# A hybrid decoder layer: the products of C and B of all groups in one place, and two attention pairs' transposes ahead of the next scores

## The chip, the cores and the metric

The kernel runs on one core of one Trainium2 chip. The metric is the device time of one execution in microseconds. Each of the core's engines runs its own queue in order and meets the others at semaphores: TensorE (PE; its weight loads are listed as PEld), VectorE (DVE), ScalarE (ACT), GpSimd (POOL) and SyncE (SP). Here SyncE only issues the loads of weights.

## The reference

One layer over 256 tokens of width 1024, in float32: a SwiGLU block, a mixer, a second SwiGLU block, with RMSNorm ahead of and behind each. The change lies in the mixer, which has two branches that share one input projection:

```python
z, xbc, dt_raw, q, k, v, gate_logits = split(u @ w_in)
# branch 1: state-space duality, in 2 chunks of 128 tokens, 4 groups of 8 heads
xs, bm, cm = split(silu(causal_dwconv(xbc)))
CB = einsum('bclgn,bcsgn->bgcls', C, B)          # per group g and chunk c
y_diag = einsum('bgcls,bgecls,bcsgep->bclgep', CB, Lmat, X)
# branch 2: differential attention, 8 heads with 2 maps each
p = softmax(q @ k.T * scale - slopes * dist)     # causal
out = (p[:, :, 0] - lam * p[:, :, 1]) @ v
out = rmsnorm(out, subln_g) * (1 - lam_init)
merged = gates[0] * (y_ssd @ w_a) + gates[1] * (out @ w_b)
h = h + rmsnorm(merged @ w_out)
```

Two steps matter here. `CB` is, for each of the four groups, a product of that group's C and B (128 states) for all pairs of tokens; the kernel computes the two diagonal blocks and the one below the diagonal. The attention's output of a pair of heads has to be transposed, so that it can be the stationary operand of its output projection.

## The kernel before, in words

**Large products.** All weights are streamed from memory in chunks of 1 MB. Each chunk is split into a high part (ScalarE, L168) and a low part (VectorE, L171) of a faster 32-bit format, and each large product is the sum of three: high by high, low by high and high by low (`mm_t` at L197, `mm_nat` at L225). Three chunks are split ahead of the one in use. The mixer's chunks come in this order: V, B and C, X (8 chunks, tile `pxs`), Z (8, `pz`), Q and K (8), the gates (8, `pgt`), the first branch's projection (8, `pws`), the second's (4, `pwd`), the output's (4). A chunk of the X stage is 48 products of 256 columns; a half-chunk of the later stages is 12 products of 512 columns.

**Small products.** Between the large ones TensorE has small ones in plain float32, each of which shows as two rows in the trace: the products of C and B (`pcb`, L865 and L866), the transposes of X (`px`) and the products of a group (`py`), and in attention the scores (`psc`, L986 and L987), the transposes of the weights of a head (`pa`, L1021), the values (`po`, L1033 to L1035) and the transposes of a pair's output (`pto`, L1060). Their results share a pool of five PSUM buffers with the tag `bg` (L84); the large products have three of their own, with the tag `pj` (L77). A tile that finds no free buffer waits until the last reader of an older tile is done.

**What sets the order.** The small work is written as generators: `cb_work` (L862), `ssd_work` (L875), `ssd_norm` (L924) and `att_work` (L1077). Each yields an estimate in microseconds after a step. A `Background` (L1109) takes steps from the first generator in its list while it has credit; the main program gives it credit after each chunk or half-chunk (`back.run`, 0.4 after an X chunk, 1.35 or 1.55 after a half-chunk of the gates and of the first branch's projection). A `BREAK` ends a call early. So the estimates decide between which large products the small ones stand. TensorE's order is the order of the program from there on; ScalarE's and VectorE's orders are chosen by the framework's scheduler.

**The products of C and B before.** One step of `cb_work` is one group: a new `bg` tile, its two products, VectorE's multiplication with the causal mask (L867), and an estimate of 0.5. With 0.4 of credit after each X chunk, one group runs after each of the first four X chunks. B and C come from a convolution (`conv`, L822): ScalarE's first tap (L826), VectorE's three further taps (L829), and ScalarE's Silu (L261). C's second half, which groups 2 and 3 read, is the last one to come out of it before X.

**Attention before.** `att_work` runs in rounds n = 0 to 5 over pairs of heads. A round has, where they exist: the scores and the softmax of pair n; the transposes of pair n-1's weights; the combination of the two maps of pair n; then, after a break, the values of pair n-1 and the norm of its output (`Pair.norm`, L1044); and last the transposes of pair n-2's output (`Pair.turn`, L1056), which ScalarE (L1072) and VectorE (L1073) read out as the high and low operand of the projection.

Of the kernel before, what the change touches and what calls it, by code (L numbers as in the profile page):

```python
# [24 lines left out]
P = 128  # L25
# [6 lines left out]
H_ATT = 8  # L32
# [16 lines left out]
def tile_hybrid_layer(ctx: ExitStack, tc: tile.TileContext, x, ffn1_pre_g, ffn1_w_gate, ffn1_w_up,  # L49
# [4 lines left out]
    nc = tc.nc  # L54
# [5 lines left out]
    def k4(shape, name, dt=F32):  # L60
        return sb.tile(shape, dt, tag="k4", name=name, bufs=K4_BUFS)
# [21 lines left out]
    def bg(shape, name):  # L83
        return ps.tile(shape, F32, tag="bg", name=name, bufs=5)  # L84
# [166 lines left out]
    order = mybir.DependencyInfo(mybir.DependencyClass.NoSync, mybir.DependencyReason.DATA)  # L251
# [68 lines left out]
    for name, v in (("mx", mix_pre_g), ("f2", ffn2_pre_g),  # L320
                    ("ng", ssd_norm_g), ("cb", ssd_conv_b), ("sg", da_subln_g)):
        n = v.shape[1] // P
# [447 lines left out]
    for jj in range(2):  # L770
        for a in (uh, ul):
            for i in range(4):
                k = i * 2 + jj
                nc.tensor.matmul(pdt[i * H_SSD:(i + 1) * H_SSD, :], wdt[:, k, :], a(k).bitcast(F32),
                                 start=jj == 0 and a is uh, stop=jj == 1 and a is ul)
# [73 lines left out]
    bT = k4([P, 4, T], "bT")  # L849
    cT = k4([P, 4, T], "cT")  # L850
# [9 lines left out]
    cbm = [cbm2[g // 2][:, g % 2, :] for g in range(4)]  # L860

    def cb_work():  # L862
        for g in range(4):
            pc = bg([P, 3 * P], f"pcb{g}")
            nc.tensor.matmul(pc[:, P:], bT[:, g, :P], cT[:, g, :], start=True, stop=True)  # L865
            nc.tensor.matmul(pc[:, :P], bT[:, g, P:], cT[:, g, P:], start=True, stop=True)  # L866
            nc.vector.tensor_tensor(cbm[g], pc, m3.rearrange("p a b -> p (a b)"), ALU.mult)  # L867
            yield 0.5

# [207 lines left out]
    def att_work():  # L1077

        pairs = [Pair(hp) for hp in range(H_ATT // 2)]
        heads = [Head(hd, pairs[hd // 2]) for hd in range(H_ATT)]
        for n in range(H_ATT // 2 + 2):
            here, old = heads[2 * n:2 * n + 2], heads[2 * n - 2:2 * n] if n else []
            for head in here:
                head.scores()
            for head in here:
                head.softmax()
                yield 2.3
            for head in old:  # L1090
                head.turn()
            if old and opens:
                opens.pop()()
            for head in here:
                head.combine()
                yield 1.3
            yield BREAK
            if old:
                for head in old:
                    head.values()  # L1100
                pairs[n - 1].norm()
                yield 1.8
                if n == H_ATT // 2:
                    yield BREAK
            if n >= 2:
                pairs[n - 2].turn()
                yield 0.8

# [25 lines left out]

    back = Background()
    back.add(cb_work())
    for g in range(4):
        xs[g] = k4([P, 4, T], f"xs{g}")
# [19 lines left out]
    for c in range(4):  # L1158
# [11 lines left out]
        back.run(BG_US)  # L1170

    back.add(att_work())


# [126 lines left out]
```

## Time and profile before

| | |
|---|---|
| time, median of 3 runs | 743.7 us (743.64 to 743.83) |
| the profiled execution, device time | 743.95 us |
| its span in the profile | 742.2 us |
| TensorE busy | 734.1 us (99%) |
| VectorE busy | 525.2 us (71%) |
| ScalarE busy | 441.1 us (59%) |
| GpSimd busy | 38.0 us (5%) |
| read from memory | 136.17 MB, 185 GB/s over the span |
| the products of C and B | between 249.0 and 269.1 us of the span |
| the transposes of pairs' outputs | between 470.0 and 505.2 us of the span |

The profile shows one execution. A row of its order of time gives the start in microseconds from the span's start, the duration in microseconds, the engine, the line of the kernel, the operation, the tile that is written and those that are read, the shape, and the number of instructions that are merged into the row; in brackets, the time that the engine sat idle before it and what ended that. A matrix product's duration overlaps with the next one's, so what a product costs is read from the distance between starts. A row of the list of waits gives who waited for whom: microseconds in total, times, and the longest.

### The profile page before, as it was taken

To read this page: it belongs to the slowest core of one execution; us is meant where nothing else is said; L and a number is where in the kernel's file an instruction comes from. 1 tells how busy PE (TensorE), PEld (TensorE's weight loads), DVE (VectorE), ACT (ScalarE), POOL (GpSimd) and SP (SyncE) were. 2 spreads that over 40 slices of the span, in tenths; PEclk is the share of its full clock that TensorE was granted. 3 is DMA by queue.
4 is the path that set the end of the run, shared out by engine and by line. 5 is a ranking of instruction groups with operands and counts; after the bars stand their busy time and mean duration, and the time that the engine had idled before them with its cause. 6 is when DMAs were issued, how large, how long until landed. Compare 5 with 4: busy or idle time off the path is not lost.

```text
span 742.2 us, 11061 instructions
## 1 busy us (share of the span) xinstructions
PE 734.1 (99%) x4369; PEld 641.7 (86%) x4369; DVE 525.2 (71%) x807; ACT 441.1 (59%) x742; POOL 38.0 (5%) x72
## 2 busy tenths in 40 slices
PE   8999999999999999999999999999999999999996
PEld 7888888888889999999999888888888888888885
DVE  6986567654577888787878997684775857766612
ACT  6665557553566565959957656772664655665512
POOL 2700000000300000000000000000020000000000
PEclk9999999999999999999999999999999999999998
DMA  8884666487253647666556455374470777645701
GB/s 291 232 261 150 213 227 254 170 286 226 64 169 118 192 150 225 191 186 223 170 161 217 165 178 213 118 244 182 140 243 15 227 226 227 193 172 185 273 1 57
DMA packets 94212, 137.96 MB, mean 186 GB/s; under 512 B 2684, under 2 KB 68304, under 8 KB 94160
## 3 DMA queue, kind: packets, MB, share of 16 engines
q1 hardware_dynamic: 91488, 129.51, 53.0%
q0 software_dynamic: 2368, 7.22, 3.1%
q8 instruction: 34, 0.56, 0.3%
q10 hardware_dynamic: 304, 0.53, 0.2%
q14 instruction: 18, 0.15, 0.1%
HBM read 136.17 MB, written 1.08 MB: 185 GB/s over the span
## 4 chain that ended last, share of the span: by engine, by line
PE 98%; DMA 1%; issue 0%; DVE 0%; SPq 0%; DVEq 0%; ACT 0%
PE acc_f L470 16%; PE pup_f L219 9%; PE pg_f L219 9%; PE pws L234 6%; PE pgt L234 6%; PE pg_f L218 4%; PE pup_f L218 4%; PE pn_f L244 3%; PE pn_f L234 3%; PE acc_mx L470 3%; PE pn_mx L234 3%; PE pwd L234 3%; PE pz L205 2%; PE pxs L207 2%; PE pz L207 2%; PE pxs L205 2%
## 5 line engine op out<-in xcount | busy, mean ns | idle before, releaser
L171 DVE TENSOR_TENSOR wlo<-raw,whi 128x1024 fp32r<-128x1024 f32 (+1 forms) x246 | 291.0, 1212 | 56.1 <-ACT whi L168 54.8
L168 ACT CAST whi<-raw 128x1024 fp32r<-128x1024 f32 (+1 forms) x245 | 246.8, 1045 | 55.4 <-PE acc_f L470 19.6
L219 PE MATMUL pg_f<-u_f,whi 128*128 128x512 f32 x288 | 101.3, 396 | 0.0
L219 PE MATMUL pup_f<-u_f,whi 128*128 128x512 f32 x288 | 101.1, 396 | 0.0
L218 PE MATMUL pg_f<-u_f,wlo 128*128 128x256 f32 x252 | 70.6, 280 | 0.0
L218 PE MATMUL pup_f<-u_f,wlo 128*128 128x256 f32 x252 | 70.3, 279 | 0.0
L219 PEld LDWEIGHTS pg_f<-u_f,whi 128*128 128x128 f32 x288 | 52.8, 188 | 9.7
L219 PEld LDWEIGHTS pup_f<-u_f,whi 128*128 128x128 f32 x288 | 52.7, 188 | 9.8
L470 PE MATMUL acc_f<-whi,gh_f 128*128 128x512 f32 x176 | 58.2, 390 | 0.0
L470 PE MATMUL acc_f<-whi,gl_f 128*128 128x512 f32 x176 | 58.1, 389 | 0.0
L470 PE MATMUL acc_f<-wlo,gh_f 128*128 128x512 f32 x176 | 58.1, 389 | 0.0
L218 PEld LDWEIGHTS pg_f<-u_f,wlo 128*128 128x128 f32 x252 | 47.5, 189 | 1.8
L218 PEld LDWEIGHTS pup_f<-u_f,wlo 128*128 128x128 f32 x252 | 47.5, 189 | 1.6
L223 DVE TENSOR_TENSOR su_f<-pup_f,su_f 128x256 f32<-128x256 f32 x36 | 15.2, 422 | 40.4 <-ACT su_f L222 40.4
L470 PEld LDWEIGHTS acc_f<-whi,gl_f 128*128 128x128 f32 x176 | 33.0, 188 | 6.9
L470 PEld LDWEIGHTS acc_f<-wlo,gh_f 128*128 128x128 f32 x176 | 33.0, 188 | 6.8
L470 PEld LDWEIGHTS acc_f<-whi,gh_f 128*128 128x128 f32 x176 | 33.0, 188 | 6.8
L234 PE MATMUL pgt<-whi,u_mx 128*128 128x512 f32 x128 | 33.1, 393 | 0.0
L222 ACT COPY su_f<-pup_f 128x256 f32<-128x256 f32 x36 | 13.4, 372 | 31.4 <-PE pup_f L219 31.1
L204 PE MATMUL pxs<-u_mx,whi 128*128 128x256 f32 x128 | 31.7, 285 | 0.0
L205 PE MATMUL pz<-u_mx,whi 128*128 128x256 f32 x128 | 31.6, 284 | 0.0
L204 PE MATMUL pz<-u_mx,whi 128*128 128x256 f32 x128 | 31.6, 284 | 0.0
(310 smaller groups left out, 1432.7 us busy)
## 6 DMA issues: line engine op xcount, KB each, us to landing
raw<-in_w_in_dram SPq DMA_DIRECT2D x40, 1024.0 KB, 5.4
raw<-in_ffn_w_down_dram SPq DMA_DIRECT2D x22, 1024.0 KB, 5.5
raw<-in_ffn_w_gate_dram SPq DMA_DIRECT2D x20, 1024.0 KB, 5.7
raw<-in_ffn_w_up_dram SPq DMA_DIRECT2D x20, 1024.0 KB, 5.4
raw<-in_ssd_w_branch_dram SPq DMA_DIRECT2D x8, 1024.0 KB, 5.0
acb<-acd POOLq DMA_DIRECT2D x8, 512.0 KB, 5.3
raw<-in_da_w_branch_dram SPq DMA_DIRECT2D x4, 1024.0 KB, 5.1
raw<-in_w_out_dram SPq DMA_DIRECT2D x4, 1024.0 KB, 5.0
```

The source lines that it names most:

```text
L168: copy(hi[:, js, :], r[:, q * nj + j:q * nj + j + n, :])
L171: nc.vector.tensor_sub(lo[:, js, :], r[:, q * nj + j:q * nj + j + n, :], hi[:, js, :].bitcast(F32))
L204: nc.tensor.matmul(acc[m], wh(j)[:, cs], ah(k0 + j), start=first and j == ks[0], stop=False)
L205: nc.tensor.matmul(acc[m], wh(j)[:, cs], al(k0 + j), start=False, stop=False)
L207: nc.tensor.matmul(acc[m], wl(j)[:, cs], ah(k0 + j), start=False, stop=last and j == ks[-1])
L218: nc.tensor.matmul(acc[:, :T], wl(j)[:, cs], ah(j), start=False, stop=False)
L219: nc.tensor.matmul(acc, wh(j)[:, cs], ahl(j), start=j == 0, stop=j == KD - 1)
L222: nc.scalar.copy(dst[:, m, :], acc[:, T:])
L223: nc.vector.tensor_tensor(dst[:, m, :], acc[:, :T], dst[:, m, :], ALU.add)
L234: nc.tensor.matmul(acc, a(k0 + j), b(j), start=first and i == 0, stop=last and i == 11)
L244: nc.tensor.matmul(accs[b], x_(k0 + j), w_(j), start=first and j == 0 and w_ is wh and x_ is acts[b][0], stop=last and j == 3 and w_ is wl)
L470: nc.tensor.matmul(acc[b][q], x_[:, ts], w_(kt)[:, halves[q]], start=i == 0 and kt == 0 and x_ is ah and w_ is wh, stop=i == n - 1 and kt ...
```

## The change

The products of C and B: `cb_work` now takes all four `bg` tiles first and issues the eight products one behind the other, held in that order by dependencies without a semaphore; then come the four masks, each with the same estimate of 0.5 as before.

Attention: for rounds 3 and 4 the transposes of pair n-3 stand at the start of the round, ahead of the scores, and no longer at the end of the round before. An estimate of 0.8 after them is gone, and the estimate after each of the two softmaxes is 2.7 in place of 2.3 from round 3 on. Pairs 2 and 3 are transposed at the end of rounds 4 and 5, as before.

```diff
     def cb_work():
-        for g in range(4):
-            pc = bg([P, 3 * P], f"pcb{g}")
-            nc.tensor.matmul(pc[:, P:], bT[:, g, :P], cT[:, g, :], start=True, stop=True)
-            nc.tensor.matmul(pc[:, :P], bT[:, g, P:], cT[:, g, P:], start=True, stop=True)
+        pcs = [bg([P, 3 * P], f"pcb{g}") for g in range(4)]
+        last = None
+        for g, pc in enumerate(pcs):
+            for m in (nc.tensor.matmul(pc[:, P:], bT[:, g, :P], cT[:, g, :], start=True, stop=True),
+                      nc.tensor.matmul(pc[:, :P], bT[:, g, P:], cT[:, g, P:], start=True, stop=True)):
+                if last is not None:
+                    tc.add_manual_dep(m.ins, last.ins.name, order, reason="together")
+                last = m
+        for g, pc in enumerate(pcs):
             nc.vector.tensor_tensor(cbm[g], pc, m3.rearrange("p a b -> p (a b)"), ALU.mult)
             yield 0.5
...
         for n in range(H_ATT // 2 + 2):
             here, old = heads[2 * n:2 * n + 2], heads[2 * n - 2:2 * n] if n else []
+            if 3 <= n <= H_ATT // 2:
+                pairs[n - 3].turn()
             for head in here:
                 head.scores()
             for head in here:
                 head.softmax()
-                yield 2.3
+                yield 2.3 if n < 3 else 2.7
...
-            if n >= 2:
+            if n >= H_ATT // 2:
                 pairs[n - 2].turn()
                 yield 0.8
```

## The prediction

> **What bounds the kernel now.** I read the page's first part, the slices and the chain that ended last, and then the list of waits for TensorE alone.
>
> ```profile
> span 742.2 us, 11061 instructions
> PE 734.1 (99%) x4369; PEld 641.7 (86%) x4369; DVE 525.2 (71%) x807; ACT 441.1 (59%) x742; POOL 38.0 (5%) x72
> ...
> PEclk9999999999999999999999999999999999999998
> ...
> PE 98%; DMA 1%; issue 0%; DVE 0%; SPq 0%; DVEq 0%; ACT 0%
> ```
>
> ```profile
> PE warm L310 <- POOL ident L296: 1.6, 1, 1.6
> PE pn_f L244 <- DVE whi L168: 0.2, 1, 0.2
> ```
>
> TensorE holds 98% of the chain at the full granted clock, and the only two waits that the list has for it lie in the first microseconds. So a microsecond taken from TensorE's own stream, or a wait put into it, goes straight to the end; what moves on VectorE and ScalarE costs nothing until TensorE waits for it. The question is therefore what TensorE's stream saves, and which dependency that had slack is now met too early.
>
> **What the change does to the queues.** I compared the instruction order in which the two programs are built. TensorE's order differs in two places alone: the products of C and B of groups 1, 2 and 3 (L865, L866) move up behind those of group 0, and the scores of heads 6 and 7 (L986, L987) move up over one half-chunk of 12 products (L234), so that they follow pair 0's transposes (L1060) directly. The transposes of pairs 1, 2 and 3 stay where they were, so most of the second part's wording changes nothing. Counts are the same: no instruction is added or removed. POOL's and SyncE's orders are the same, so no DMA is moved past another. VectorE and ScalarE change in a few neighbouring places in the two stretches.
>
> **Part 1: the four groups together, what it saves.** TensorE's order of time around group 0, then the starts of groups 1 and 2, then a stretch without such a group:
>
> ```profile
> 249.03 0.60 PE L865 MATMUL pcb<-cT,bT 128*128 128x256 f32 x2
> 249.47 0.38 PE L866 MATMUL pcb<-cT,bT 128*128 128x128 f32 x2
> ...
> 249.81 0.28 PE L205 MATMUL pxs<-u_mx,whi 128*128 128x256 f32 x1
> ...
> 255.44 0.60 PE L865 MATMUL pcb<-cT,bT 128*128 128x256 f32 x2
> ...
> 261.85 0.60 PE L865 MATMUL pcb<-cT,bT 128*128 128x256 f32 x2
> ...
> 273.70 1.12 PE L207 MATMUL pxs<-u_mx,wlo 128*128 128x256 f32 x8
> 276.58 1.12 PE L207 MATMUL pxs<-u_mx,wlo 128*128 128x256 f32 x8
> ```
>
> Without a group, 24 products take 276.58 - 273.70 = 2.88 us, 0.12 each, so a full chunk of 48 takes 5.76. With one it takes 255.44 - 249.03 = 6.41. A group costs 0.65. Its own stream is 0.44 (249.03 to 249.47) for the two wide passes and 0.22 for the two narrow ones (the price of two narrow passes in the order of time below, 469.79 to 470.01), together 0.66. So going into the group and back costs nothing that these rows show, and three exits fewer save 0.00. The upper bound of a switch is the 0.09 of part 2.
>
> **Part 1: the wait it adds.** Group 2 reads the second half of C. It is final after its Silu (L261), which stands in ScalarE's queue behind the first step of the next convolution (L826); the third row is from the order of weight loads:
>
> ```profile
> 249.23 0.57 ACT L826 ACTIVATE xs<-pxs,cols_a,cols_b 128x256 f32<-128x256 f32 x1 [1.90 <-PE pxs L207]
> 249.70 0.62 ACT L261 ACTIVATE cT<-cT 128x512 f32<-128x512 f32 x1
> ...
> 249.69 0.19 PEld L205 LDWEIGHTS pxs<-u_mx,whi 128*128 128x128 f32 x1
> ```
>
> The Silu ends at 249.70 + 0.62 = 250.32. Before, group 2 ran at 261.85 and had 11 us to spare; now its first product comes at 249.03 + 2 x 0.65 = 250.33, and its weight load, which carries the wait, starts some 0.11 earlier (a load at 249.69 for the product of 249.81 shows that lead in the rows after the group), at 250.22. A release takes 0.05:
>
> ```profile
> 574.94 0.69 DVE L573 TENSOR_TENSOR sg_f2b<-pn_f,sg_f2b 128x512 f32<-128x512 f32 x1
> ...
> 575.68 0.66 PE L581 MATMUL pt_f<-ident,sg_f2b 128*128 128x128 f32 x4
> ```
>
> (VectorE ends at 575.63, TensorE starts at 575.68). So the load starts at 250.37 instead of 250.22: +0.15. Ends: 0 if that Silu ends 0.15 sooner, and 0.4 if the load is no longer hidden behind a product (0.19 on top). I take 0.15. Behind it wait groups 2 and 3 and the next chunk of X; VectorE's masks (L867) come earlier than before, and the chunks after group 3's old place are at their old time again, so weight splits only gain time.
>
> **Part 2: what it saves.** TensorE's order of time around pair 0's transposes:
>
> ```profile
> 469.79 0.39 PE L1035 MATMUL po<-v,aT 128*128 128x128 f32 x2
> 470.01 0.60 PE L1060 MATMUL pto<-ident,o 128*128 128x128 f32 x4
> 470.37 1.16 PE L234 MATMUL pws<-whi,yh 128*128 128x512 f32 x4
> ...
> 472.27 1.07 PE L234 MATMUL pws<-whi,yl 128*128 128x512 f32 x4
> 473.27 0.50 PE L986 MATMUL psc<-k,q 64*128 64x128 f32 x4
> ...
> 474.03 0.49 PE L986 MATMUL psc<-k,q 64*128 64x128 f32 x4
> ...
> 474.88 1.21 PE L234 MATMUL pws<-whi,yh 128*128 128x512 f32 x4
> ...
> 477.78 1.07 PE L234 MATMUL pws<-whi,yh 128*128 128x512 f32 x4
> ...
> 480.50 1.07 PE L234 MATMUL pws<-whi,yh 128*128 128x512 f32 x4
> ```
>
> Four products of 512 columns take 0.907 (a third of the 2.72 that 12 take from 477.78 to 480.50). The 12 products from 470.37 to 472.27 + 0.91 = 473.18 take 2.81, so leaving the transposes for products cost at most 0.09; most of that is only the first row being stamped early. The scores start 0.09 after 473.18 because their tile changes to 64 rows; that price stays, whatever stands ahead. One exit fewer saves between 0 and 0.09; I take 0.05.
>
> **Part 2: the wait it adds.** The small products share a pool of five buffers (tag bg, L84). In the changed order six of them stand in a row: po of pair 1, pto of pair 0, then the four score tiles of heads 6 and 7. The last one (head 7, second map) must take a buffer back, and in the built program it takes pto's and waits for its last reader, VectorE's L1073 (L1078 in the changed kernel). It did so before as well, but 12 products stood between. The readers:
>
> ```profile
> 470.70 0.68 ACT L1072 ACTIVATE oh<-pto,g 128x512 fp32r<-128x512 f32 x1
> ```
>
> ```profile
> 469.61 1.23 DVE L171 TENSOR_TENSOR wlo<-raw,whi 128x1024 fp32r<-128x1024 f32 x1 [5.97 <-ACT whi L168]
> ...
> 471.44 0.74 DVE L1073 SCALAR_TENSOR_TENSOR ol<-pto,g,oh 128x512 fp32r<-128x512 f32 x1
> ...
> 472.36 2.36 DVE L171 TENSOR_TENSOR wlo<-raw,whi 128x1024 fp32r<-128x1024 f32 x2
> 474.63 0.69 DVE L1054 TENSOR_TENSOR o<-po,ro 128x512 f32<-128x512 f32 x1
> 475.24 0.68 DVE L1216 TENSOR_TENSOR gt<-pws,gt 128x512 f32<-128x512 f32 x1
> 475.83 1.48 DVE L993 SCALAR_TENSOR_TENSOR s<-dneg,psc 128x384 f32<-128x384 f32 x3
> 477.22 0.95 DVE L996 TENSOR_REDUCE nm<-s 128x6 f32<-128x768 f32 x1
> ```
>
> Everything up to L1073 keeps its place in both queues, so it still ends at 471.44 + 0.74 = 472.18 and frees TensorE at 472.23. TensorE is there earlier: transposes end at 470.01 + 4 x 0.11 = 470.45, the tile change adds 0.09, head 6 runs 470.54 to 471.30 (0.76, as 473.27 to 474.03), and head 7's second map would start at 471.31. It waits 0.92. Its four passes then run alone; before, both maps of head 7 shared 0.85 (474.03 to 474.88), and one alone needs between 0.66 (0.22 + 0.44, the group of part 1) and that. So the next product starts between 472.89 and 473.08, and with the transition at 0.09 between 472.98 and 473.08, against 470.54 + 1.61 = 472.15 without a wait: +0.83 to +0.93. I take 0.88. Low end: 0, if L1073 is done in time; high end 1.9, if one ScalarE cast (1.05, the slow rival).
>
> What is late next? VectorE now takes the new scores and the norm before two weight subtractions and before the eviction of the half-chunk (L1216). From 472.25: two scores 0.9 (two thirds of 477.22 - 475.83), the norm 0.6, a maximum 0.9, two subtractions 2.3 and the eviction 0.6 end at about 477.6. TensorE wants that buffer at the product of 480.50, now about 481.5: 3.9 us of cover, and the weight halves that now end some 2 us later are read only after it. Without that cover each extra subtraction would cost its 1.15.
>
> **Sum.** -0.00 +0.15 -0.05 +0.88 = +0.98, say 1.0 us. The profiled execution took 743.95 for its span of 742.2; it becomes 744.95. That execution lies 0.25 above the median of 743.7, so the median becomes 744.7: 0.13% slower, which is inside the 0.2% (1.5 us) that a measurement of this kernel tells from no change.
>
> One rule speaks against this change as a whole. The rows first; in the last, the granted clock is the 1.00 behind the five engines' busy times:
>
> ```profile
> 311.58 2.82 PE L913 MATMUL py<-E,X 128*64 128x256 f32 x32
> 314.33 1.09 PE L881 MATMUL px<-ident,xs 128*128 128x128 f32 x8
> ...
> 311.00:316.00 5.00, 4.98 (x52) 4.02 (x51) 4.15 (x8) 3.79 (x5) 0.00 (x0) 1.00 0.87 257
> ```
>
> A run of small products and transposes of 3.8 us (311.58 to 315.4) left the granted clock at 1.00 in that window. The Trainium skill's page "TensorE: Matmul & The Clock Gate" says in Part 1 that TensorE falls to half its clock after an idle window of about 3.4 us, and in Part 4 that transposes do not count as busy in the same way. By the rows the sum has no term for it; by that rule the longer run here might add an estimated 1.7 us (half of one such window).
>
> **The rivals.**
> (a) The wait at head 7 is not there, because L1073 has already ended: 743.7 + 0.15 - 0.05 = 743.8. Against it: L1073 needs ScalarE's L1072, which cannot start before the transposes end at 470.45 and took until 471.38; then 0.74 alone gives 472.1.
> (b) Slower by more than 0.2%: one 1.05 us cast (L168) comes ahead of L1072, because ScalarE is that much later against TensorE than in this execution, and head 7 waits 1.05 more: 745.8. It decides from 0.5 us of slip on. For it: VectorE's row of 469.61 waited 5.97 us for ScalarE, so this stretch hangs on ScalarE; against it: the order of both queues up to L1073 is fixed and unchanged.
> (c) The clock falls. The run of small work becomes at least 469.79 to 473.0 with a 0.9 us wait in it. If the products after it ran at half speed for as long as that run lasted (3.2), 1.6 us are lost: 746.3. The window from 311 to 316 speaks against it. This is the rule of the Trainium skill's page "TensorE: Matmul & The Clock Gate" that stands above.
> (d) Faster by more than 0.2%: every exit from small products costs far more than the rows say. It takes 1.5 us on four exits, plus the 1.0 of waits: 0.6 each against 0.09 at most; 742.0.
>
> **How the numbers follow.** The forecast has 0.62 (its own range 744.3 to 745.1), (a) 0.12, (b) 0.14, (c) 0.04, (d) 0.05, and 0.03 for another wait that makes it slower. Forecast and (a) are within 0.2%: 0.74. (b), (c) and the rest are slower: 0.21. (d) is faster: 0.05. The range takes in (a) with both savings at their upper bound (743.7 less four exits at 0.09) and (b): 743.3 to 745.9.
>
> **What would show it.** In the profile after: four rows of L866 and L867 in one stretch from 249.03 to about 251.8; a wait of TensorE's pcb on ScalarE's cT of 0.1 to 0.4; a wait of psc on VectorE's L1078 of about 0.9 near 471.4; the granted clock at 1.00; no other wait of TensorE's. The prediction is wrong if that second wait is missing or longer than 1.4, if the clock drops after 473, or if a group of L866 and L867 costs less than 0.6.

## The result: 1.1 us slower, as forecast

The changed kernel takes 744.89 us (median of 20 runs, 744.64 to 745.48). The kernel before takes 743.77 us beside it (median of 20 runs, 743.51 to 744.42). The ratio is 1.0015, with a 95% interval of 1.0009 to 1.0022: 1.12 us or 0.15% slower, where the prediction had 1.0 us and 0.13%. That is inside the 0.2% that the prediction treated as no change, but the interval excludes an equal time.

The page of the changed kernel has the lines that answer to those shown of the kernel before:

```profile
span 742.9 us, 11061 instructions
PE 734.9 (99%) x4369; PEld 642.6 (86%) x4369; DVE 525.6 (71%) x807; ACT 440.8 (59%) x742; POOL 37.9 (5%) x72
...
PEclk9999999999999999999999999999999999999999
...
PE 96%; ACT 1%; DVE 1%; DMA 0%; issue 0%; DVEq 0%
```

TensorE still bounds the kernel, at the full granted clock. What is new is in the last line: the chain that ended last was 98% TensorE before and is 96% now, and for about 1% each it passes through ScalarE and VectorE. All of that is one detour of 18.7 us. In order of time (start, duration, engine, tile and line), its first piece off TensorE, its last one, and the return:

```profile
453.36 1.03 DVE s L998 x2
...
471.34 0.67 DVE ol L1078
...
472.05 0.48 PE psc L991 x2
```

So the share does not tell the size of a wait. The chain shows one wait of TensorE, which ends at 472.05. It is followed back from there through the queues of VectorE and ScalarE, of which only the last microsecond is time that TensorE waited. Around the products of C and B the chain stays on TensorE. The list of waits for TensorE's products has no new row; it has a single one, from the first microseconds:

```profile
PE warm L310 <- POOL ident L296: 1.6, 1, 1.6
```

The weight loads have a list of their own, and there the wait at 472.05 does stand; the list before has no such row:

```profile
PEld psc L991 <- DVE ol L1078: 0.5, 1, 0.5
```

**How the two traces were compared.** Since TensorE's stream is nearly gapless, the distance between the first products of two stages tells what a stage took. The first products of X (`pxs`), of the first branch's projection (`pws`) and of the second's (`pwd`), in TensorE's order of time, before:

```profile
243.27 0.28 PE L204 MATMUL pxs<-u_mx,whi 128*128 128x256 f32 x1
...
449.65 0.70 PE L234 MATMUL pws<-whi,yh 128*128 128x512 f32 x2
...
504.92 0.71 PE L234 MATMUL pwd<-whi,oh 128*128 128x512 f32 x2
```

and after:

```profile
242.93 0.28 PE L204 MATMUL pxs<-u_mx,whi 128*128 128x256 f32 x1
...
449.46 0.70 PE L234 MATMUL pws<-whi,yh 128*128 128x512 f32 x2
...
505.64 0.71 PE L234 MATMUL pwd<-whi,oh 128*128 128x512 f32 x2
```

From `pxs` to `pws`, which holds part 1 of the change, it is 206.38 before and 206.53 after: +0.15. From `pws` to `pwd`, which holds part 2, it is 55.27 and 56.18: +0.91. Together +1.06 us. What lies behind is the same to 0.01 us. What lies ahead is the start-up, which in these two executions happens to be 0.35 shorter after; this is why the profiled span has grown by only 0.7 (1.06 - 0.35). Over many runs that evens out, and the medians are 1.12 apart.

**Part 1.** TensorE's order of time in the changed kernel (L866 and L867 are the old L865 and L866):

```profile
248.69 0.60 PE L866 MATMUL pcb<-cT,bT 128*128 128x256 f32 x2
249.13 0.38 PE L867 MATMUL pcb<-cT,bT 128*128 128x128 f32 x2
249.35 0.60 PE L866 MATMUL pcb<-cT,bT 128*128 128x256 f32 x2
249.78 0.38 PE L867 MATMUL pcb<-cT,bT 128*128 128x128 f32 x2
250.03 0.70 PE L866 MATMUL pcb<-cT,bT 128*128 128x256 f32 x2
250.56 0.38 PE L867 MATMUL pcb<-cT,bT 128*128 128x128 f32 x2
250.79 0.60 PE L866 MATMUL pcb<-cT,bT 128*128 128x256 f32 x2
```

and the Silu of C's second half, in ScalarE's:

```profile
249.36 0.62 ACT L261 ACTIVATE cT<-cT 128x512 f32<-128x512 f32 x1
```

The first group takes 0.66 to the start of the second (248.69 to 249.35). Group 2 starts at 250.03, 0.05 after the Silu's end at 249.98, and takes 0.76 to the next, of which its first row took 0.53 (250.03 to 250.56) where the others take 0.43 or 0.44. The wait shows as a late start (0.02 later than 249.35 + 0.66) and a slower first product, not as idle time: the modelled end of the product before, 249.78 + 0.38 = 250.16, lies beyond it.

**Part 2.** TensorE's order of time around pair 0's transposes, after:

```profile
469.60 0.39 PE L1040 MATMUL po<-v,aT 128*128 128x128 f32 x2
469.82 0.60 PE L1065 MATMUL pto<-ident,o 128*128 128x128 f32 x4
470.35 0.50 PE L991 MATMUL psc<-k,q 64*128 64x128 f32 x4
470.68 0.61 PE L992 MATMUL psc<-k,q 64*128 64x256 f32 x4
471.11 0.38 PE L991 MATMUL psc<-k,q 64*128 64x128 f32 x2
471.33 0.59 PE L992 MATMUL psc<-k,q 64*128 64x256 f32 x2
472.05 0.48 PE L991 MATMUL psc<-k,q 64*128 64x128 f32 x2
472.38 0.59 PE L992 MATMUL psc<-k,q 64*128 64x256 f32 x2
472.90 1.20 PE L234 MATMUL pws<-whi,yh 128*128 128x512 f32 x4
```

and the two readers of pair 0's transposes, on ScalarE and VectorE:

```profile
470.52 0.68 ACT L1077 ACTIVATE oh<-pto,g 128x512 fp32r<-128x512 f32 x1
```

```profile
471.26 0.74 DVE L1078 SCALAR_TENSOR_TENSOR ol<-pto,g,oh 128x512 fp32r<-128x512 f32 x1
```

The count at the end of a `psc` row is what to look at. Head 6 has rows of 4: the products of its two maps run side by side (in the trace each product of the second map starts 0.01 after its partner of the first). Head 7 has rows of 2: its first map runs at 471.11 and 471.33 alone, its second only at 472.05, 0.05 after L1078 has ended (471.26 + 0.74 = 472.00). So head 7 takes 1.79 (471.11 to 472.90) where it took 0.85 before.

### The profile page after: what moved, and what is told of

It is laid out like the page before. It is cut to its first block, busy times and chain, and to the rows that moved or that the text cites. A ratio compares the mean times of both kernels' runs of the same rounds, so it can differ in the third digit from the quotient of the medians.

```text
span 742.9 us, 11061 instructions
## 1 busy us (share of the span) xinstructions
PE 734.9 (99%) x4369; PEld 642.6 (86%) x4369; DVE 525.6 (71%) x807; ACT 440.8 (59%) x742; POOL 37.9 (5%) x72
## 4 chain that ended last, share of the span: by engine, by line
PE 96%; ACT 1%; DVE 1%; DMA 0%; issue 0%; DVEq 0%
PE acc_f L470 16%; PE pup_f L219 9%; PE pg_f L219 9%; PE pgt L234 6%; PE pws L234 4%; PE pg_f L218 4%; PE pup_f L218 4%; PE pn_f L244 3%; PE pn_f L234 3%; PE acc_mx L470 3%; PE pn_mx L234 3%; PE pwd L234 3%; PE pz L205 2%; PE pxs L204 2%; PE pxs L207 2%; PE pxs L205 2%
```

## The experiments

The theory is that both costs are waits for a reader or a writer that is late, and that joining the small products saves next to nothing. The main rival: the exits from small to large products cost more than the rows told, so that joining does save something, and the waits cost correspondingly more than forecast. In the table, the stretches are read from first rows like those above; each kernel was profiled once, and the same stretch of the same order repeats to about 0.02, as the last section shows, so a difference of 0.02 is at the edge of what they tell. The medians are beside 743.7 to 744.0 of the kernel before in the same sets of runs, where there was a set. Beside the two late readers and the scattered products the kernel before ran only once and took 746.47, so the times of those single runs say nothing, and only their stretches are used.

| kernel | median, us | ratio to before (95%) | `pxs` to `pws` | `pws` to `pwd` |
|---|---|---|---|---|
| before | 743.77 | | 206.38 | 55.27 |
| after | 744.89 | 1.0015 (1.0009 to 1.0022) | 206.53 | 56.18 |
| groups alone | 743.78 | 1.0000 (0.9991 to 1.0009) | 206.53 | 55.28 |
| pairs alone | 744.87 | 1.0010 (1.0001 to 1.0019) | 206.39 | 56.17 |
| both, without the waits | 743.81 | 0.9999 (0.9990 to 1.0008) | 206.41 | 55.25 |
| after, sixth buffer | 744.10 (one run) | | 206.54 | 55.21 |
| after, late reader | 745.11 (one run) | | 206.54 | 56.71 |
| before, late reader | 743.96 (one run) | | 206.37 | 55.28 |
| before, products scattered | 743.49 (one run) | | 206.35 | 55.27 |
| scattered, and sixth buffer | 743.72 | 0.9999 (0.9991 to 1.0008) | 206.35 | 55.22 |

**One part at a time.** The first kernel has the new `cb_work` and the old `att_work`, the second the old `cb_work` and the new `att_work`; there is no other edit.

> Part 1 alone: the eight products of C and B together after the first X chunk, attention as before. Two stretches of TensorE's stream are read: X, from the first pxs product to the first pz product (48.67 us before, 48.83 with the whole change), and A, from the first pws product to the first pwd product (55.28 before, 56.17 with the whole change). My theory (the wait for C's second half, 0.15): X 48.83, A 55.28, time 0.1 to 0.2 us above before. Rival (the grouping shifts VectorE's and ScalarE's work and that carries into attention): A longer than 55.5 and time about 1 us above before.

> Part 2 alone: pair transposes moved, C and B group by group as before. My theory (head 7's second map waits 0.9 us for the buffer of pair 0's transposes): X 48.67, A 56.17, time 0.9 us above before. Rival (the two parts act on each other, each is free alone): A 55.3 and no difference in time.

Each stretch changed only with its own part (206.53 and 56.17), and by the same amount as in the changed kernel. The parts do not act on one another. The medians agree: 743.78 with part 1 alone, 744.87 with part 2 alone; on its own, part 1's 0.15 is too little for a median to show.

**Both parts without their waits.** The four groups stay together but run one X chunk later, when C's second half has long been final; pair 0's transposes join the small products that come after the next scores, so that the scores do not take their buffer back.

```diff
     def cb_work():
+        yield 0.5
         pcs = [bg([P, 3 * P], f"pcb{g}") for g in range(4)]
...
-            if 3 <= n <= H_ATT // 2:
-                pairs[n - 3].turn()
             for head in here:
                 head.scores()
...
             for head in old:
                 head.turn()
+            if 3 <= n <= H_ATT // 2:
+                pairs[n - 3].turn()
```

> Both regroupings at places where nothing is waited for: the eight products of C and B together, but one X chunk later; pair 0's transposes behind the transposes of heads 4 and 5 instead of ahead of the scores, so that the scores follow pair 1's values directly. The number of exits from small products is the same as in the changed kernel, four fewer than before. My theory (the two waits are the whole cost and an exit saves between 0 and 0.09): X 48.67, A 55.2 to 55.3, time 0 to 0.2 us below before, not to be told from it. Rival that exits cost 0.4 each: X 47.5, A 54.9, time 1.5 us below before. Rival that moving the scores up costs by itself: A 56.1.

Both stretches are back within 0.03 of before (206.41 and 55.25), while the joining remains. The loss is the two waits. Group 2 follows group 1 after 0.66 here and takes 0.65 itself (256.64 to 257.29 us), although the four groups take four buffers in a row as in the changed kernel. That speaks for the Silu, and against a buffer, as what it waited for there. The joining itself costs 0.03 in the one stretch and saves 0.02 in the other, little more than the stretches scatter.

**A sixth buffer.** The changed kernel, with one of the six `bg` tiles in a row taken from the large products' pool instead:

```diff
-            self.psc = [bg([P, 3 * P], f"psc{hd}{m}") for m in range(2)]
+            self.psc = [pj(f"psc{hd}{m}")[:, :3 * P] if (hd, m) == (6, 0) else bg([P, 3 * P], f"psc{hd}{m}")
+                        for m in range(2)]
```

> The changed kernel with one edit: the first of the four score tiles of heads 6 and 7 comes from the pool of the large products, where one of three buffers is free at that time, so that the fourth needs no buffer back. TensorE's order is that of the changed kernel. My theory (the buffer is the wait): A 55.2 to 55.3 in place of 56.17, X 48.83 as in the changed kernel. Rival (the cost lies in the scores' tile change right behind the transposes, or in the order itself): A 56.1.

TensorE's order of time in that kernel (L991 and L992 have become L992 and L993):

```profile
470.25 0.60 PE L1066 MATMUL pto<-ident,o 128*128 128x128 f32 x4
470.78 0.50 PE L992 MATMUL psc<-k,q 64*128 64x128 f32 x4
471.10 0.61 PE L993 MATMUL psc<-k,q 64*128 64x256 f32 x4
471.54 0.49 PE L992 MATMUL psc<-k,q 64*128 64x128 f32 x4
471.76 0.70 PE L993 MATMUL psc<-k,q 64*128 64x256 f32 x4
472.39 1.19 PE L234 MATMUL pws<-whi,yh 128*128 128x512 f32 x4
```

The order of the products is that of the changed kernel; only the buffer differs. Both heads have rows of 4 again, and head 7 takes 0.85 (471.54 to 472.39). Against the changed kernel the stretch is 0.97 shorter (56.18 - 55.21), which is what running out of buffers cost. Against the kernel before it is 0.06 shorter; the kernel without the waits, with as many exits, was 0.02 shorter. So the one exit fewer is worth 0.02 to 0.06.

**The late reader made later.** VectorE's readout of pair 0's transposes is done twice, the second time writing the same values again; once in the changed kernel, once in the kernel before.

```diff
             nc.vector.scalar_tensor_tensor(lo, pt, g8, hi.bitcast(F32), ALU.mult, ALU.subtract)
+            if hp == 0:
+                nc.vector.scalar_tensor_tensor(lo, pt, g8, hi.bitcast(F32), ALU.mult, ALU.subtract)
```

> The changed kernel with VectorE's reading of pair 0's transposes done twice, so that the buffer comes free about 0.65 us later. My theory: head 7's second map waits 0.65 longer, A 56.8 (56.17 before this edit). Rival (the cost is the order or the tile change, not the buffer): A 56.2.

> The kernel before with the same second reading on VectorE. My theory: with 12 products between the transposes and the scores the later release is still in time (about 472.8 of the span against 474.0), A 55.28 as before. Rival (VectorE, busy for 7.96 of the 8 us from 475 on, is the bound here): A 55.9.

In the kernel before nothing moved (55.28): there, 12 products cover the readout. In the changed kernel the stretch grew by 0.53, and not for the reason given. The list of waits for TensorE and VectorE's order of time in that kernel:

```profile
PE psc L991 <- DVE s L998: 0.7, 1, 0.7
```

```profile
471.22 0.74 DVE L1078 SCALAR_TENSOR_TENSOR ol<-pto,g,oh 128x512 fp32r<-128x512 f32 x1
471.95 0.54 DVE L998 SCALAR_TENSOR_TENSOR s<-dneg,psc 128x384 f32<-128x384 f32 x1
472.41 0.74 DVE L1080 SCALAR_TENSOR_TENSOR ol<-pto,g,oh 128x512 fp32r<-128x512 f32 x1
```

Head 7's second map started at 472.54. That is 0.05 after L998 ended (471.95 + 0.54 = 472.49), and well before the second reading, L1080, ended at 473.15. So the sixth tile no longer waits for the transposes' buffer but for that of a map of head 6, whose reader is L998; in the program as built it is the first map's. The run does not price the second reading, and the expectation failed in its reason. What it does show is a second case of the same wait: with another of the five buffers the sixth tile again waits for a readout by VectorE, and restarts 0.05 after it.

**Many more exits in the X stage.** In the kernel before, each of the eight products of C and B runs behind an X chunk of its own, so that there are eight exits instead of four.

```diff
             nc.tensor.matmul(pc[:, P:], bT[:, g, :P], cT[:, g, :], start=True, stop=True)
+            yield 0.4
             nc.tensor.matmul(pc[:, :P], bT[:, g, P:], cT[:, g, P:], start=True, stop=True)
             nc.vector.tensor_tensor(cbm[g], pc, m3.rearrange("p a b -> p (a b)"), ALU.mult)
-            yield 0.5
+            yield 0.4
```

> The kernel before with each of the eight products of C and B behind an X chunk of its own: eight places in place of four, so four more exits from small products. My theory (an exit in this stretch costs nothing): X 48.67, at most 49.0 by the upper bound of 0.09. Rival (an exit costs 0.4): X 50.2.

Around the first of them:

```profile
248.64 0.60 PE L865 MATMUL pcb<-cT,bT 128*128 128x256 f32 x2
248.88 0.47 PE L204 MATMUL pxs<-u_mx,whi 128*128 128x256 f32 x1
249.19 0.28 PE L205 MATMUL pxs<-u_mx,whi 128*128 128x256 f32 x1
249.31 0.28 PE L204 MATMUL pxs<-u_mx,whi 128*128 128x256 f32 x1
```

From 248.64 to 249.19 there is one small product and one of the X products, which are 0.12 apart: the small one cost 0.43, no more than it costs in the middle of a group (0.44). The whole stretch is 0.03 shorter than before, not longer. So an exit costs nothing that shows in this stage, and part 1 had nothing to save.

**The best of both.** Scattered products, and the second part of the change with the sixth buffer:

> The eight products of C and B each behind an X chunk of their own, and the second part of the change with a buffer of the large products for one score map. If the stretches of TensorE's stream add up as they did so far: from the first pxs to the first pws product 0.03 us less than before (206.35 against 206.38), from the first pws to the first pwd product 0.06 us less (55.21 against 55.27), all other stretches behind the start-up equal to 0.02; together 0.09 us less than before, 0.01%. That is far inside the scatter of the start-up, so the median should stand within 0.2% of the one before, with an interval that takes in no change. Rival: the stretches do not add up, since moving single products also moves the readers of the bg tiles; then the second stretch is longer than 55.25 and a wait of psc or pws shows in it.

The stretches add up as before (206.35 and 55.22), 0.08 us less in all than in the kernel before. The median is 743.72 beside 743.70. By its trace this order is the shortest of all, 0.01% less than the kernel before, but no measured time here can tell it from the kernel before, so it is no improvement that has been shown.

## Why the prediction was right, step by step

- **Part 1, saving** (0.00): right. Joined without the wait, the products make their stretch 0.03 longer than before; scattered, 0.03 shorter. There is nothing to save.
- **Part 1, wait** (+0.15): right in its mechanism: the Silu of C's second half ends at 249.98, group 2 starts 0.05 later, and the same 0.05 stands in the traces of the three other kernels with this order (groups alone, sixth buffer, late reader). The size is 0.12 (206.53 - 206.41, with the joining the same and the wait gone). That the stretch grew by just 0.15 is this and the 0.03 of the joining, which the prediction put at nothing, so the exact hit is partly luck.
- **Part 2, saving** (0.05 of 0 to 0.09): right, 0.06 measured with the sixth buffer and 0.02 with the waits taken out.
- **Part 2, wait** (0.88 of 0.83 to 0.93): the mechanism was right, down to the row it restarts on; the size came out at 0.97, just above the range. The wait itself is as forecast (0.92): side by side with the first map, which starts at 471.11, the second would have started 0.01 later, at 471.12 (as the maps of head 6 do), and it starts at 472.05, which makes 0.93. The term that was a little short is what follows: the second map alone, from 472.05 to the next large product at 472.90, takes 0.85, where the step allowed 0.75 to 0.85 (472.23 to between 472.98 and 473.08) and took the middle. The upper value was right: here one map alone took as long as two side by side (0.85 with the sixth buffer). From the transposes to the next large product the wait costs 0.94 (469.82 to 472.90, against 470.25 to 472.39 with the sixth buffer). The other 0.03 of the 0.97 lie behind that product, in the rest of the stretch; what they are stays open.
- **What is late next** (VectorE's eviction of the half-chunk, 3.9 us of cover): right. The eviction, L1216 then and L1223 now, is the first row, and the product that needs the buffer the second:

```profile
476.71 0.68 DVE L1223 TENSOR_TENSOR gt<-pws,gt 128x512 f32<-128x512 f32 x1
```

```profile
481.21 1.07 PE L234 MATMUL pws<-whi,yh 128*128 128x512 f32 x4
```

It ends at 477.39 and has 3.8 us of cover; no third wait appeared.

- **The sum** (+0.98): +1.06 in the stream, +1.12 in the medians.
- **The rivals.** (a) and (b) fell with the row of 472.05: the wait was there, and L1077 was not delayed. (d) fell with the measured time and with the scattered products; its own figure should have been 742.2 (743.7 - 1.5) in place of 742.0. (c), the clock, fell with the row of stretches of the changed kernel, in which the granted clock stands behind the five engines' busy times:

```profile
469.00:477.00 8.00, 7.88 (x47) 6.22 (x47) 7.57 (x12) 5.62 (x15) 0.00 (x0) 1.00 0.41 133
```

The clock stayed at 1.00 through 3 us of small products with that wait of 0.93 us in it. The Trainium skill's page "TensorE: Matmul & The Clock Gate" says in Part 4 that transposes do not count as busy in the same way. The trace does not test this: its four transposes here take 0.44 us (4 x 0.11).

One sign that the prediction named came only in part: it said that the two waits would show as waits of `pcb` (0.1 to 0.4) and of `psc` on L1078 (about 0.9). The second is listed under the weight loads, which by the prediction's own words carry the wait, but with 0.5 only; the first is in neither list. The distances between starts have both in full. The row above shows why the list for products is silent: of the wait at head 7 (0.93) it has 0.12 as idle (8.00 - 7.88), since the modelled end of the first map's last row, 471.33 + 0.59 = 471.92, lies just ahead of the restart at 472.05.

## What to carry to other kernels

Before moving small products together, count the tiles in a row against the buffers of their pool: the first tile too many waits until another engine has read out an older one (here 0.93 us), unless enough other products stand in between (here 12 products did, 2.7 us). What joining can save is read from the rows before: a group's distance between starts less the price of its own passes, which here was nothing. And a product that had microseconds to spare behind its input may have none in its new place, so look up when each input is final before moving its reader.

## What the runs showed of the hardware that was not expected

TensorE's stream repeats far better than the measured time. Between executions of the ten kernels, stretches that an edit doesn't touch agree to about 0.02 us over 55 to 206 us, while the first product of the first large stage starts anywhere between 30.35 (pairs alone) and 31.31 us (both, without the waits). The waits of TensorE in the latter kernel:

```profile
PE pn_f L244 <- DVE whi L168: 0.7, 1, 0.7
PE pn_f L244 <- DVE raw_u L363: 0.3, 1, 0.3
```

These lie in the start-up; the changed kernel's list has neither of them. So the ten profiled executions differ, apart from what the edits do, by their first 31 us; that the unprofiled runs scatter for the same reason is likely but not shown. And a change of 0.1 us in the middle, which no set of medians here could show, can be read from one profiled execution each.

A wait of 0.93 us on the engine that bounds the kernel can be missing from the list for its products, where modelled ends of earlier products cover it, and stand in the list for its weight loads with 0.5 only. The one in the late-reader kernel, half a microsecond longer, is listed with 0.7 in the first and with 1.1 in the second. So both lists are to be asked, and the size is to be read from distances between starts.
